# Seven block products in the first MLP, and its modulation sums moved from VectorE to ScalarE and GpSimd

## The chip, the cores and the metric

The kernel runs on one core of a Trainium2 chip. The metric is the device time of one execution in microseconds (us). The core's engines are called here by the profile's names: PE is TensorE (matmuls; PEld its weight loads), DVE is VectorE, ACT is ScalarE, POOL is GpSimd, and SP is SyncE, which here only issues DMA transfers. Each engine works through its own instructions in a fixed order and waits on semaphores for the others.

## What is computed

Two transformer blocks run one after the other on x (512 tokens, 1024 wide, float32). In outline:

```python
# first block
x = x + attention_one(rmsnorm(x, attn_norm_g)) @ w_out
hid = square(relu(rmsnorm(x, mlp_norm_g) @ w_up))      # 512 x 4096
x = x + hid @ w_down                                   # the product that is changed
# second block: six modulation rows of x's condition c, and two of the context's
mod_x = silu(c) @ w_mod + b_mod                        # 1024 x 6144
mod_c = silu(c_ctx) @ w_mod + b_mod
x = x + gt1 * rmsnorm(mix(modulate(x), modulate(ctx)) @ w_out_2)
x = x + gt2 * rmsnorm(square(relu(modulate(x) @ w_mlp_in)) @ w_mlp_out)
```

All matmuls are float32 to almost full precision: each operand is split in a high and a low part, and three matmuls (high by high, high by low, low by high) add up in PSUM.

## The kernel before

**Order.** The phases follow each other: `attention_one`, `dense_one` (the output projection, the first block's MLP, and beside it the modulation rows and the context's keys and values), `attention_two`, `dense_two` (the second projection and MLP). A scheduler lays the instructions of each engine in a fixed order, ahead of the run, by a model of their durations; work of a later part that is ready may stand before work of an earlier one. Nothing is reordered on the chip. SP issues nearly all loads, in one queue; POOL issues the small transfers and the spills.

**Splits.** `split` (L147, L148) copies a tile on ACT to its high part and subtracts on DVE to get the low part. Weights come 512 KB at a time in one of two raw buffers, and their two parts go into rings of five tiles, `wh` and `wl` (`weights`, `fetch` L169, `parts`). `mm3` (L152 to L154) issues the three matmuls. For the first four up tiles of an MLP, POOL does the low part (`WPJ`).

**First block's MLP (`mlp`).** The 4096 hidden columns are 32 tiles of 128, in four groups of eight. `up(j)` makes one tile: 24 matmuls of 512 columns (the first five in two halves of 256), ReLU on ACT (L843), the square on DVE (L844), and a split. After eight of them a down phase multiplies the group by its rows of `w_down`: four token tiles by two halves of the output, 192 matmuls. `evac2` (L975, DVE) adds each result, times the square of the norm's factor, to x, which stays in SBUF (`xa`).

**Modulation (`mods`).** A generator that `extra` advances two steps after each up tile and each eviction. A step loads 128 rows by 1024 columns of `w_mod` (L893) into one of two buffers and adds them, scaled by silu(c), to an accumulator on DVE (L896 the first, L898 the others); for the first two of six column blocks there is a second accumulator for the context. A finished accumulator is split, summed over partitions by matmuls with ones (L910, L911), gets its bias (L912) and gain (L916) on DVE, and goes to DRAM through POOL's queue (L906, L915, L918).

**Second block's MLP (`mlp_seven`).** For three of its four groups the down product is done in seven block products (Strassen's scheme in Winograd's form): hidden tiles and tokens form a 2 x 2 block matrix, rows of `w_mlp_out` and output halves another. DVE makes four sums of hidden blocks per pair of tiles (L1301 to L1304) and the splits are longer; POOL makes the differences of weight blocks (L1365, `less`), eight of 128 x 1024 in a group; seven products of 24 matmuls each go to PSUM pairs and from there to sums Y (L1355 on ACT in the first group, L1357 on DVE after that). At the end `join` (L1389, POOL) makes the four output blocks of the sums. The last group is plain.

## Time and profile before

| | |
|---|---|
| median of 3 runs | 1255.91 us (1252.36 to 1256.43) |
| the profiled execution's own time | 1260.07 us |
| its span in the trace | 1258.3 us, 16992 instructions |
| HBM | 143.24 MB read, 6.36 MB written, 119 GB/s over the span |
| first block's MLP in the trace | 277 to 661 us |
| second block's MLP in the trace | 903 to 1254 us |

Times in the trace count from the start of the span. A line number such as L148 is a line of the kernel; a helper that many parts call, as `split`, has one line for all, and there the tile's name tells the parts apart (m1u is the first MLP's up weight, m1d its down weight, m1hid its hidden tile, m2 the second's; the ending h or l is the high or low part). Matmuls overlap in PE's pipeline, so the length of one is more than the distance to the next. The chain of work that ended last is a PE chain through the second MLP.

### The profile page before, as it was taken

How to read it: one execution, taken by the hardware profiler on the slowest of the kernel's cores; microseconds unless marked ns; L12 is line 12 of the kernel's file. 1: busy time of each engine (PE TensorE's matmuls, PEld its weight loads, DVE VectorE, ACT ScalarE, POOL GpSimd, SP SyncE). 2: the span in 40 equal slices, each digit the busy share in tenths (PEclk: the TensorE clock that was granted, in tenths of full speed). 3: DMA queues.
4: the chain of work that ended last, by engine and by line, in shares of the span. 5: the costliest groups of instructions: out<-in, count | busy, mean ns of one | idle time of the engine just before them, and what ended most of it. 6: DMA issues, size and time to landing. Idle time of an engine off the chain costs nothing. (4 is left out here: it accounts for less than half of the span.)

```text
span 1258.3 us, 16992 instructions
## 1 busy us (share of the span) xinstructions
PE 1213.5 (96%) x6316; PEld 1017.5 (81%) x6316; DVE 844.6 (67%) x1410; ACT 567.3 (45%) x1068; POOL 355.1 (28%) x370
## 2 busy tenths in 40 slices
PE   7899999999999999999999999999899999999997
PEld 6898888779888878888889878777798888888885
DVE  3799766597898854346355557574868678777744
ACT  5576656434223313225254546463546454343431
POOL 2787552252010000000014124030642504205502
PEclk9899999999999999999999999999999999999999
DMA  6222222365678734134145311215443643524421
GB/s 165 64 60 53 57 63 68 101 183 154 197 220 258 240 119 138 67 101 135 67 151 157 84 53 52 85 38 201 124 162 102 185 123 117 147 81 134 150 68 67
DMA packets 151707, 150.71 MB, mean 120 GB/s; under 512 B 14345, under 2 KB 115480, under 8 KB 151624
## 3 DMA queue, kind: packets, MB, share of 16 engines
q1 hardware_dynamic: 147224, 139.41, 36.4%
q0 software_dynamic: 4400, 10.22, 2.6%
q8 instruction: 49, 0.80, 0.3%
q14 instruction: 34, 0.28, 0.1%
HBM read 143.24 MB, written 6.36 MB: 119 GB/s over the span
## 5 line engine op out<-in xcount | busy, mean ns | idle before, releaser
L1365 POOL TENSOR_TENSOR m2d<-m2d,m2d 128x1024 f32<-128x1024 f32 x24 | 71.2, 2981 | 162.2 <-DVE m2w220l L148 51.5
L898 DVE SCALAR_TENSOR_TENSOR macc<-mod,silu_c,macc 128x1024 f32<-128x1024 f32 x56 | 76.1, 1369 | 15.5 <-DMA mod<-in_w_mod_dram 15.2
L975 DVE SCALAR_TENSOR_TENSOR xa<-m1d,r,xa 128x512 f32<-128x512 f32 x32 | 23.8, 746 | 37.5 <-PE m1d L154 37.5
L918 POOL DMA_DIRECT2D modrows<-mrow x8 | 3.9, 492 | 146.4 <-DVE mrow L916 91.9
L147 ACT ACTIVATE m2hid<-m2sq 128x512 fp32r<-128x512 f32 (+1 forms) x32 | 17.6, 551 | 49.1 <-DVE m2sq L1328 49.1
L147 ACT ACTIVATE m1hid<-m1sq 128x512 fp32r<-128x512 f32 x32 | 20.0, 630 | 38.3 <-DVE m1sq L844 38.3
L148 DVE TENSOR_TENSOR npl<-t,nph 128x512 fp32r<-128x512 f32 x32 | 21.7, 682 | 16.4 <-ACT nph L147 16.3
L194 POOL TENSOR_SCALAR p<-p,d 128x512 f32<-128x512 f32 x8 | 14.0, 1752 | 57.1 <-DVE d L1116 27.3
L148 DVE TENSOR_TENSOR m2hid<-m2sq,m2hid 128x512 fp32r<-128x512 f32 (+1 forms) x32 | 24.3, 760 | 6.0 <-ACT m2hid L147 5.8
L181 POOL TENSOR_SCALAR w<-w,g_attn 128x384 f32<-128x384 f32 x20 | 25.8, 1297 | 9.1 <-DMA w<-in_w_in_dram 6.7
L148 DVE TENSOR_TENSOR m1hid<-m1sq,m1hid 128x512 fp32r<-128x512 f32 x32 | 22.0, 687 | 9.1 <-ACT m1hid L147 9.1
L683 DVE TENSOR_REDUCE mb<-sb 128x1 f32<-128x128 f32 (+3 forms) x32 | 15.6, 487 | 16.5 <-PE sb L680 16.4
L1115 ACT ACTIVATE p<-s,m 128x512 f32<-128x512 f32 x32 | 22.0, 688 | 5.8 <-DVE m L1113 5.8
L1069 POOL TENSOR_TENSOR tb<-G,nam 128x256 f32<-128x256 f32 x24 | 17.8, 774 | 22.1 <-DVE m L1109 12.5
L685 ACT ACTIVATE pb<-sb,mb 128x128 f32<-128x128 f32 (+3 forms) x32 | 16.8, 525 | 16.0 <-DVE mb L683 15.7
L843 ACT ACTIVATE m1re<-m1up 128x512 f32<-128x512 f32 x32 | 18.6, 583 | 10.1 <-PE m1up L154 9.8
L204 POOL TENSOR_SCALAR nc_0ss<-nc_0ss 128x1 f32<-128x1 f32 x1 | 0.2, 187 | 80.5 <-ACT nc_0x L256 80.5
L152 PE MATMUL pj<-w_0h,xnT 128*128 128x384 f32 (+1 forms) x48 | 18.0, 376 | 4.9 <-ACT pjs L407 3.9
L147 ACT ACTIVATE nph<-t 128x512 fp32r<-128x512 f32 x32 | 19.0, 595 | 7.5 <-PE t L1126 7.2
L981 POOL DMA_DIRECT2D xspill<-xa x4 | 2.6, 655 | 70.0 <-DVE xa L975 69.9
L844 DVE SCALAR_TENSOR_TENSOR m1sq<-m1up,m1re 128x512 f32<-128x512 f32 x32 | 21.8, 683 | 0.1
L1328 DVE SCALAR_TENSOR_TENSOR m2sq<-m2up,m2sq 128x512 f32<-128x512 f32 x32 | 21.9, 684 | 0.0
(2017 smaller groups left out, 4679.7 us busy)
## 6 DMA issues: line engine op xcount, KB each, us to landing
mod<-in_w_mod_dram SPq DMA_DIRECT2D x48, 512.0 KB, 4.6
m2d<-in_w_mlp_out_dram SPq DMA_DIRECT2D x44, 512.0 KB, 3.7
m1u<-in_w_up_dram SPq DMA_DIRECT2D x32, 512.0 KB, 4.3
m1d<-in_w_down_dram SPq DMA_DIRECT2D x32, 512.0 KB, 3.6
m2u<-in_w_mlp_in_dram SPq DMA_DIRECT2D x32, 512.0 KB, 4.1
w<-in_w_in_dram SPq DMA_DIRECT2D x16, 512.0 KB, 4.2
w<-in_w_in_dram SPq DMA_DIRECT2D x48, 128.0 KB, 2.6
o1w<-in_w_out_dram SPq DMA_DIRECT2D x8, 512.0 KB, 3.8
```

The lines of the kernel that those rows point to most:

```text
L147: self.nc.scalar.activation(out=hi, in_=src, func=AF.Copy)
L148: (eng or self.nc.vector).tensor_tensor(out=lo, in0=src, in1=hi.bitcast(F32), op=ALU.subtract)
L152: mm(out=out, lhsT=lh, rhs=rh, start=start, stop=False)
L181: eng.tensor_scalar(out=rv[:, i], in0=rv[:, i], scalar1=g, scalar2=None, op0=ALU.mult)
L843: ac(out=r, in_=acc, func=AF.Relu)
L844: nc.vector.scalar_tensor_tensor(out=s, in0=acc, scalar=0.0, in1=r, op0=ALU.max, op1=ALU.mult)
L898: nc.vector.scalar_tensor_tensor(out=accs[s], in0=rw, scalar=sc[:, s, k:k + 1], in1=accs[s], op0=ALU.mult, op1=ALU.add)
L975: nc.vector.scalar_tensor_tensor(out=x[t][:, cols], in0=acc, scalar=r2[:, t:t + 1], in1=x[t][:, cols], op0=ALU.mult, op1=ALU.add)
L1069: nc.gpsimd.tensor_tensor(out=tb[:, h, y], in0=G[:, h, ::-1, o:o + 32][:, :, ::-1], in1=nam[:, y, :].unsqueeze(1).to_broadcast([P, 8, 32]) ...
L1115: ac(out=pr, in_=s, func=AF.Exp, bias=m[:, 2:3], accum_out=den[:, 0:1])
L1328: nc.vector.scalar_tensor_tensor(out=s, in0=acc, scalar=0.0, in1=s, op0=ALU.max, op1=ALU.mult)
L1365: pt(out=o, in0=x, in1=z, op=ALU.subtract)
```

## The change

The first block's MLP now goes through `mlp_seven` too, which both blocks share in a new form; the old `mlp` goes away. With that:

- Three of the first block's four groups use seven products; the last group is plain. The evictions of a group go to sums Y in SBUF instead of x; product 1 is added to two sums, and `joined` needs ten additions on POOL instead of fourteen. The operand sums are made in place.
- To make room, x is written to DRAM after the output projection and comes back (four loads of 512 KB) during the last group, where DVE adds the sums to it.
- The modulation works in twelve column blocks of 512 instead of six of 1024, with four buffers. ACT scales each loaded tile and POOL adds it to the accumulator. `extra` advances the generator three steps, after each up tile and each product's eviction.
- During the first MLP the products have PSUM banks 0 to 3, transposes and modulation bank 4, and the up tiles 5 to 7.
- In the first MLP the weight blocks have five buffers (`RB_1`), in the second six (`RB_2`, as before).

Parts that are written but not used by this kernel (`last_seven`) are left out here.

```diff
@@ constants
+MRAW = 4
+RB_2 = 6
+RB_1 = 5
+MSTEPS = 3
@@ mods
+        def raw(name):
+            return ep.tile([P, 512], F32, tag="mraw", name=name, bufs=MRAW)
...
-        for cb in range(6):
+        for blk in range(12):
+            cb, hf = blk // 2, blk % 2
...
-                rw = ep.tile([P, D], F32, tag="mraw", name=f"mod{cb}{k}", bufs=2)
-                nc.sync.dma_start(out=rw, in_=a["w_mod_2"][0, k * P:(k + 1) * P, cb * D:(cb + 1) * D])
+                rw = raw(f"mod{blk}{k}")
+                nc.sync.dma_start(out=rw, in_=a["w_mod_2"][0, k * P:(k + 1) * P, wcols])
                 for s in range(len(accs)):
+                    gain = sc[:, s, k:k + 1]
                     if k == 0:
-                        nc.vector.tensor_scalar(out=accs[s], in0=rw, scalar1=sc[:, s, k:k + 1], scalar2=None, op0=ALU.mult)
-                    else:
-                        nc.vector.scalar_tensor_tensor(out=accs[s], in0=rw, scalar=sc[:, s, k:k + 1], in1=accs[s],
-                                                       op0=ALU.mult, op1=ALU.add)
+                        ac(out=accs[s], in_=rw, func=AF.Copy, scale=gain)
+                        continue
+                    term = raw(f"term{blk}{k}") if s + 1 < len(accs) else rw
+                    ac(out=term, in_=rw, func=AF.Copy, scale=gain)
+                    nc.gpsimd.tensor_tensor(out=accs[s], in0=accs[s], in1=term, op=ALU.add)
                 yield
...
@@ dense_one, evac1
+                    nc.gpsimd.dma_start(out=self.xspill[t * P:(t + 1) * P, :], in_=x[t])
...
+        self.banks(a=(0, 1, 2, 3), t=(4,), s=(5, 6, 7))
...
+    def mlp_one(self, hT, g, r2):
...
+        def extra():
+            for _ in range(MSTEPS):
+                next(gen, None)
+        last_ups, last_plain, _ = self.mlp_seven(hT, a["w_up"], a["w_down"], hidx, Y, RB_1, extra, "m1")
+        for _ in gen:
+            pass
...
+            if j == NJ - 4:
+
+                for t in range(NT):
+                    x[t] = xtile(f"xa2{t}")
+                    nc.sync.dma_start(out=x[t], in_=self.xspill[t * P:(t + 1) * P, :])
+                    for half in range(2):
+                        cols = slice(half * 512, half * 512 + 512)
+                        nc.vector.scalar_tensor_tensor(out=x[t][:, cols], in0=Y[((2, 3), (4, 5))[t // 2][half]][t % 2],
+                                                       scalar=r2[:, t:t + 1], in1=x[t][:, cols], op0=ALU.mult, op1=ALU.add)
...
@@ mlp_seven
+            self.split(hi[:, 1:3].rearrange("p o t -> p (o t)"), lo[:, 1:3].rearrange("p o t -> p (o t)"), s)
+            a11, a21, a12, a22 = st[:, 0, 0:256], st[:, 0, 256:512], st[:, 1, 0:256], st[:, 1, 256:512]
+            tt(out=a22, in0=a21, in1=a22, op=ALU.add)
+            tt(out=a21, in0=a11, in1=a21, op=ALU.subtract)
+            tt(out=a11, in0=a22, in1=a11, op=ALU.subtract)
+            tt(out=a12, in0=a12, in1=a11, op=ALU.subtract)
+            self.split(hi[:, 3:7], lo[:, 3:7], st.rearrange("p f (x t) -> p (f x) t", x=2))
...
+        def down(g):
+            def into(*ns):
+                def evac(tau, acc):
+                    for n, first in ns:
+                        if g == 0 and first:
+                            ac(out=Y[n][tau], in_=acc, func=AF.Copy)
+                        else:
+                            tt(out=Y[n][tau], in0=acc, in1=Y[n][tau], op=ALU.add)
+                    extra()
+                return evac
+            b11 = blocks(g, 0, 0)
+            times(g, 1, 0, b11, into((6, True), (2, True)))
+            t1 = blocks(g, 0, 1)
+            less(t1, t1, b11)
+            times(g, 5, S1, t1, into((5, True)))
+            t2 = blocks(g, 1, 1)
+            less(t2, t2, t1)
+            times(g, 6, S2, t2, into((6, False)))
+            b21 = blocks(g, 1, 0)
+            times(g, 2, A12, b21, into((2, False)))
+            less(b21, t2, b21)
+            times(g, 4, A22, b21, into((4, True)))
+            b22 = blocks(g, 1, 1)
+            times(g, 3, S4, b22, into((3, True)))
+            b12 = blocks(g, 0, 1)
+            less(b22, b22, b12)
+            times(g, 7, S3, b22, into((7, True)))
...
+        for g in range(NG - 1):
+            for j in range(g * G, (g + 1) * G):
+                if j == NSP:
+                    self.rings["s"] = s_banks
+                up(j, True)
+                extra()
+            down(g)
```

## Rows read from the trace of the kernel before

**Rows 1.** The page's first part: busy time, share of the span, instructions.
```profile
PE 1213.5 (96%) x6316; PEld 1017.5 (81%) x6316; DVE 844.6 (67%) x1410; ACT 567.3 (45%) x1068; POOL 355.1 (28%) x370
```
**Rows 2.** Stretches: length, busy by engine (instructions), granted clock, DMA share, GB/s.
```profile
253.00:298.00 45.00, 41.85 (x246) 37.00 (x245) 37.92 (x37) 15.59 (x22) 26.03 (x20) 0.96 0.61 181
277.00:332.00 55.00, 51.85 (x342) 47.83 (x341) 48.39 (x52) 21.63 (x31) 18.20 (x17) 0.97 0.57 170
332.00:431.00 99.00, 99.00 (x426) 79.89 (x425) 81.86 (x88) 31.74 (x39) 8.21 (x14) 1.00 0.73 229
431.00:476.00 45.00, 43.19 (x179) 34.39 (x178) 29.37 (x31) 10.11 (x11) 1.94 (x4) 0.96 0.50 154
1039.00:1078.00 39.00, 39.00 (x170) 31.79 (x169) 36.34 (x30) 14.30 (x16) 22.30 (x8) 1.00 0.39 123
```
**Rows 3.** Timeline of ACT: ReLU evictions (start, length, engine, line, operation, tiles).
```profile
514.95 0.58 ACT L843 ACTIVATE m1re<-m1up 128x512 f32<-128x512 f32 x1
520.53 0.58 ACT L843 ACTIVATE m1re<-m1up 128x512 f32<-128x512 f32 x1
...
611.77 0.58 ACT L843 ACTIVATE m1re<-m1up 128x512 f32<-128x512 f32 x1
...
1122.63 0.58 ACT L1327 ACTIVATE m2sq<-m2up 128x512 f32<-128x512 f32 x1
...
1206.17 0.58 ACT L1327 ACTIVATE m2sq<-m2up 128x512 f32<-128x512 f32 x1
```
**Rows 4.** Timeline around TensorE's two waits (in brackets: idle before, what ended it).
```profile
278.33 5.69 DVE L898 SCALAR_TENSOR_TENSOR macc<-mod,silu_c,macc 128x1024 f32<-128x1024 f32 x2
...
279.60 3.34 POOL L148 TENSOR_TENSOR m1u2l<-m1u,m1u2h 128x1024 fp32r<-128x1024 f32 x1
...
284.77 0.63 PE L216 MATMUL n_2t<-ident,xg 128*128 128x128 f32 x4 [3.15 <-DVE xg L940]
...
444.42 0.50 PE L152 MATMUL m1d<-m1d100h,m1hid 128*128 128x512 f32 x1 [1.81 <-DVE xa L975]
```
**Rows 5.** Tiles macc and mrow: count, shortest/median/longest in ns, first and last start.
```profile
L898 DVE SCALAR_TENSOR_TENSOR macc<-mod,silu_c,macc x56: 1261/1278/3386, 257.4 to 448.4; 128x1024 f32<-128x1024 f32 x56
...
L906 POOL DMA_DIRECT2D mrow<-in_b_mod_dram x8: 484/490/609, 290.0 to 438.5; - x8
```
**Rows 6.** Prices: POOL's sum and difference, ACT's copy, DVE's operand sum.
```profile
L940 POOL TENSOR_TENSOR xg<-xa,g_mlp x4: 1263/1280/2277, 241.7 to 260.9; 128x512 f32<-128x512 f32 x4
...
L1365 POOL TENSOR_TENSOR m2d<-m2d,m2d x24: 2394/3261/3447, 927.4 to 1147.7; 128x1024 f32<-128x1024 f32 x24
...
L147 ACT ACTIVATE m1hid<-m1sq 128x512 fp32r<-128x512 f32 x32 | 20.0, 630 | 38.3 <-DVE m1sq L844 38.3
...
1041.02 0.42 DVE L1301 TENSOR_TENSOR g_post<-m2sq 128x256 f32<-128x256 f32 x1
```
**Rows 7.** Timeline of DVE and POOL in a down phase of the second block.
```profile
1063.53 3.04 DVE L148 TENSOR_TENSOR m2w170l<-m2d,m2w170h 128x1024 fp32r<-128x1024 f32 x1
...
1065.65 3.19 POOL L1365 TENSOR_TENSOR m2d<-m2d,m2d 128x1024 f32<-128x1024 f32 x1 [0.16 <-POOL m2d L1365]
...
1066.49 0.68 DVE L1357 TENSOR_TENSOR y<-m2p,y 128x512 f32<-128x512 f32 x1
1067.09 2.83 DVE L148 TENSOR_TENSOR m2w171l<-m2d,m2w171h 128x1024 fp32r<-128x1024 f32 x1
...
1069.35 9.52 POOL L1365 TENSOR_TENSOR m2d<-m2d,m2d 128x1024 f32<-128x1024 f32 x3 [0.52 <-DMA m2d<-in_w_mlp_out_dram]
```
**Rows 8.** Timeline: a weight split, and first uses of split weights on TensorE.
```profile
498.34 1.23 DVE L148 TENSOR_TENSOR m1d200l<-m1d,m1d200h 128x1024 fp32r<-128x1024 f32 x1 [2.30 <-ACT m1d200h L147]
...
519.60 0.40 PE L152 MATMUL m1d<-m1d200h,m1hid 128*128 128x512 f32 x1
...
1074.09 0.40 PE L152 MATMUL m2p<-m2w171h,m2hid 128*128 128x512 f32 x1
```
**Rows 9.** DMA issues: a load of 256 KB, median us to landing.
```profile
w<-in_w_in_dram SPq DMA_DIRECT2D x6, 256.0 KB, 3.9
```

More of the change, by code (lines that the diff above doesn't have):

```diff
@@ L900, in mods @@
                 yield
             for (s, gname, dst) in todo[cb]:
-                ah = self.part("wh", f"mh{cb}{s}")
-                al = self.part("wl", f"ml{cb}{s}")
-                self.split(ah, al, accs[s])
-                row = ep.tile([P, D], F32, tag="xr", name=f"mrow{cb}{s}", bufs=2)[0:1, :]
-                nc.gpsimd.dma_start(out=row, in_=a["b_mod_2"][:, cb * D:(cb + 1) * D])
-                for hf in range(2):
-                    pt = self.ps("t", f"mp{cb}{s}{hf}")
-                    cols = slice(hf * 512, hf * 512 + 512)
-                    nc.tensor.matmul(out=pt, lhsT=ones, rhs=ah[:, cols], start=True, stop=False)
-                    nc.tensor.matmul(out=pt, lhsT=ones, rhs=al[:, cols], start=False, stop=True)
-                    nc.vector.tensor_tensor(out=row[:, cols], in0=pt[0:1, :], in1=row[:, cols], op=ALU.add)
+                hl = self.part("wh", f"mh{blk}{s}")
@@ new lines, in mods @@
+                self.split(hl[:, 0:512], hl[:, 512:1024], accs[s])
+                row = raw(f"mrow{blk}{s}")[0:1, :]
+                nc.gpsimd.dma_start(out=row, in_=a["b_mod_2"][:, wcols])
+                pt = self.ps("t", f"mp{blk}{s}")
+                nc.tensor.matmul(out=pt, lhsT=ones, rhs=hl[:, 0:512], start=True, stop=False)
+                nc.tensor.matmul(out=pt, lhsT=ones, rhs=hl[:, 512:1024], start=False, stop=True)
+                nc.vector.tensor_tensor(out=row, in0=pt[0:1, :], in1=row, op=ALU.add)
@@ L924, in dense_one @@
     def dense_one(self):
[L925 to L929 removed]
+        tc, nc, a = self.tc, self.nc, self.a
         g = self.gp.tile([P, 2, D], F32, tag="g", name="g_mlp")
@@ L976, in evac2 @@
                                            op0=ALU.mult, op1=ALU.add)
-            if grp == NJ // 8 - 1 and half == 1:
+            if half == 1:
                 if t == 0:
@@ L1230, in squares @@
+    def squares(self, src, ss, second, name, tag="sqr"):
         nc = self.nc
         j = self.ep.tile([P, 512], F32, tag=tag, name=name, bufs=2)
-        nc.scalar.activation(out=j, in_=src, func=AF.Square, accum_out=ss[:, half:half + 1])
-        if half == 0:
+        nc.scalar.activation(out=j, in_=src, func=AF.Square, accum_out=ss[:, second:second + 1])
+        if not second:
             nc.gpsimd.tensor_scalar(out=ss[:, 0:1], in0=ss[:, 0:1], scalar1=1.0 / D, scalar2=EPS, op0=ALU.mult, op1=ALU.add)
@@ new lines, in dense_two @@
+            hidx = self.ep.tile([P, 7168], F32R, tag="hidx", name="m2hidx", bufs=1)
+            more = self.ep.tile([P, D], F32, tag="more", name="m2more", bufs=1)
+            Y = {n: [b[:, h * 512:h * 512 + 512] for h in range(2)]
+                 for n, b in ((2, y[0]), (3, y[1]), (4, y[2]), (5, y[3]), (6, more), (7, gg[:, 0, :]))}
+            self.row(gg[:, 1, :], 5)
+            last_ups, last_plain, last_seven = self.mlp_seven(hT, a["w_mlp_in_2"][0], a["w_mlp_out_2"][0], hidx, Y, RB_2, lambda: None, "m2")
@@ new lines, in dense_two, with fetch_x, done @@
+            x = {}
+            ss2 = [self.small("ss", f"ss2{t}") for t in range(NT)]
+            def fetch_x(ts):
+                for t in ts:
+                    x[t] = self.ep.tile([P, D], F32, tag="rb", name=f"xc{t}", bufs=RB_2)
+                    nc.sync.dma_start(out=x[t], in_=self.xspill2[t * P:(t + 1) * P, :])
+            def done(t, half, first, z):
+                r = self.squares(z, ss2[t], 0 if first else 1, f"sk{half}{t}", "sqr")
+                nc.vector.tensor_tensor(out=z, in0=z, in1=gg[:, 1, half * 512:half * 512 + 512], op=ALU.mult)
+                if not first:
+                    for _, c in self.post(x[t], [Y[((2, 3), (4, 5))[t // 2][i]][t % 2] for i in range(2)], r):
+                        nc.sync.dma_start(out=self.out[0, t * P:(t + 1) * P, c], in_=x[t][:, c])
@@ L1426, with evac @@
+            last_ups(False, lambda j: None)
+            fetch_x(range(NT))
+            def evac(half, t, acc):
+                z = Y[((2, 3), (4, 5))[t // 2][half]][t % 2]
+                nc.vector.tensor_tensor(out=z, in0=acc, in1=z, op=ALU.add)
+                done(t, half, half == 0, z)
+            last_plain(evac)
 _INS = ['x', 'attn_norm_g', 'w_in', 'b_forget', 'q_norm_a', 'k_norm_a', 'sink_logits', 'q_norm_b', 'k_norm_b', 'w_out',
```

400 lines of the change are left out of this document (182 added, 218 removed).

## The prediction

> **What bounds the kernel now.** I read the page first: TensorE is busy 96% of the span, VectorE (DVE) 67%, GpSimd (POOL) 28% [rows 1]. Shares over the span hide the stages, so I then cut the first block's MLP into stretches [rows 2]. From 332 to 431 TensorE is busy all 99 us, DVE 81.9 and POOL 8.2 of them. TensorE's matmuls set the time there, DVE is close behind, and POOL has room.
>
> TensorE's pace comes from the ReLU evictions: two neighbouring up tiles are 5.58 us apart [rows 3], and one has 24 matmuls of 512 columns, so a matmul costs 0.2325 us. From the last ReLU of one group of eight tiles to that of the next, the plain first block takes 91.24 us and the second block, with seven products, 83.54 us [rows 3].
>
> TensorE waits twice in the stretch: 3.15 us for DVE's xg and 1.81 us for DVE's eviction [rows 4]. The first shows a trap. DVE took 5.69 us for two modulation steps of 1.28 us (the median, [rows 5]) because POOL's split of m1u2, 3.34 us, ran beside them; xg stood behind them, and TensorE behind xg. The order on each engine is fixed ahead, so a collision that it does not foresee becomes a wait of this kind. The stretches around the two waits have a mean granted clock of 0.97 over 55 us and 0.96 over 45 us [rows 2], between the levels of 1.2 and 2.4 GHz, where 332 to 431 has 1.00: that is 1.65 and 1.8 us more. Together: 3.15 + 1.81 + 3.45 = 8.4 us.
>
> **The change, part by part.**
>
> *TensorE.* In three of four groups seven products of 24 matmuls replace 192: 3 x 24 x 0.2325 = 16.7 us less. The periods differ by 7.7 us a group instead of 5.58, but the plain one also holds context and modulation work and clock loss, so I keep the count.
>
> *DVE.* Removed: 64 modulation terms of at most 1.28 us [rows 5], 82 us. Added in three groups: for each of 12 pairs of tiles four operand sums of 0.42 and a split of 1.23, with 0.42 + 0.68 where 2 x 0.68 was, 2.7 us; six more weight splits of 1.23 a group; 18 more evictions and sums with x of 0.68 net (42 for 24) [rows 6 to 8]: 32 + 22 + 12 = 66 us. DVE's own work falls by only some 16 us. But the steps that held xg go, and I count the 8.4 us as gained; if other work delays the same places it is 0.
>
> *ACT.* 128 terms at 0.63 us [rows 6] are 81 us, with splits and copies of the products some 120 us. ACT was busy 31.7 + 10.1 of 144 us [rows 2]. I take 0; a term that waits for its load holds the weight splits behind it in ACT's queue, which is counted below.
>
> *POOL.* 112 sums of 1.26 us [rows 6] are 141 us, 24 differences of 2.39 us [rows 6] are 57 us, and 42 instead of 21 small transfers of 0.49 us [rows 5]; x is written out once more, four more issues.
>
> *POOL beside DVE* decides. In the second block's products the two take turns [rows 7]: DVE's split ends at 1066.57, POOL's difference, begun at 1065.65, ends 2.27 us after that, and DVE's next split ends 1.08 us after POOL. Evictions from PSUM keep 0.68 us beside POOL. So a POOL sum and a DVE instruction with two SBUF inputs exclude each other. Three turns took 9.52 us, 3.17 each, a little less than 2.27 + 1.08; scaled to that the exclusive parts are 2.15 us for a difference, 1.08 for a sum of 512, and 1.02, 0.51 and 0.26 us for DVE's 1024, 512 and 256 columns.
> - An up phase needs 8 x 1.02 + 4 x (0.26 + 0.51 + 4 x 0.26 + 1.02) = 19.5 us, a down phase 14 x 1.02 + 8 x 2.15 = 31.5 us.
> - Sums in a phase: a step with two accumulators holds two of the four buffers through a load (3.9 us, [rows 9]), 1.26 us of ACT and 2.52 of POOL, so four sums come per 7.7 us: 17 in what is left of the first up phase after 298 (33 us), 23 in the second. In a down phase POOL has 39 - 8 x 2.39 = 19.9 us, 16 sums. Before 298 it has 45 - 26.0 us [rows 2], 15 sums. The last 25 fall in the third up phase.
> - Demand against TensorE's time: first up 15.4 + 18.4 in 33; each down 31.5 + 17.3 in 39; second up 19.5 + 24.8 + 4 (accumulator splits) in 47; third up 19.5 + 27 + 4 in 44.7. Excess: 0.8 + 9.8 + 1.3 + 9.8 + 5.8 = 27.5 us.
> - What the queues carry: a weight split was done 20.0 us before its use in the plain block (499.57 to 519.60), 4.2 us in the second block's down phase (1069.92 to 1074.09) [rows 7, 8]. Both kinds of phase occur, so I take the middle, 12.1 us.
>
> That leaves 27.5 - 12.1 = 15.4 us of TensorE idle and, in the two down phases at least, clock losses of 1.73 us each: 18.9 us. Bounds: 0 where all is carried, 31 us where nothing is.
>
> The Trainium skill has this as a rule (SBUF — State Buffer, "Who interferes with whom"): the port pair that both share is an exclusive lock, and a DVE instruction with two SBUF inputs contends for it with a GpSimd one that reads SBUF. It speaks against the change, and the turns of [rows 7] agree with it.
>
> *Transfers.* 96 loads of half the size for 48, 12 more blocks of w_down and four reloads of x: 64 more issues on SP's queue. The stretch 332 to 431 had the DMA engines 0.73 busy [rows 2] with no wait of TensorE; I take 0. A load that waits for a buffer that a POOL sum frees holds the weight loads behind it: the same excess, not a second one.
>
> *Edits at nothing.* The second block's two more evictions a group, 1.36 us, fit in DVE's 36.3 of 39 us [rows 2]; without that cover up to 2.7 us. Its joins fall from 14 to 10 on POOL, a gain that I don't count. Four PSUM banks for five leave an eviction of 0.68 us one product, 5.58 us; it is late only where DVE is, which is the excess again. x comes back while three up tiles are still to run.
>
> **Sum:** -16.7 - 8.4 + 18.9 = -6.2 us. Against the profiled execution's own 1260.07 us this is 1253.9; the median of the runs is 1255.91, 4.2 us lower, so 1249.7, given as 1250 us.
>
> **Rivals.**
> - *The sums hide*: 0 for the exclusion, -25.1, 1231 us; with the old waits left, 1239. For: 81.9 of 99 us on DVE did not stop TensorE [rows 2]. Against: POOL has some 220 us to do in the stretch, and more in its turns.
> - *The gain is eaten*: the queues carry only the 4.2 us of a down phase: -25.1 + 27.5 - 4.2 + 3.5 = +1.7, 1257.6 us.
> - *Slower: the same exclusion with the sums early.* Each call hands out three steps, 113 steps in 1.7 groups. If the queues keep that pace, 97 sums (104.8 us) and 91.7 us of other demand stand in 140.5 us of TensorE from 298 to the middle of the second down phase: 56 over, 12.1 carried, 3.5 of clock: -25.1 + 47.4 = +22.3, 1278 us. It turns the sign where the excess passes 25.1 + 12.1 - 3.5 = 33.7 us. For: the old terms ran at that pace, 257.4 to 448.4 [rows 5]. Against: four buffers and POOL's own 1.26 us spread the sums.
> - *The products save less than counted* needs dearer matmuls; the 83.54 us period of the same products [rows 3] speaks against it.
>
> **How the numbers follow.** A measurement of this kernel can tell about 0.3%, 3.8 us, from no change. Chances: the forecast's zone (1241 to 1252) 0.34, hidden (below 1241) 0.14, eaten (1252 to 1260) 0.18, slower 0.34 (0.20 up to 1275, 0.14 beyond). So faster 0.48, same 0.18, slower 0.34. The range 1234 to 1280 leaves out some 0.06 below and 0.12 above; the likeliest case's own range is 1234 to 1252.
>
> **What would show it.** Right: a period near 84 us between last ReLUs of the first block once the sums are done; POOL over 0.7 busy to about 500, its sums stretched from 1.26 towards 2 us; DVE's splits of 1.23 us at 2 to 3 us; TensorE idle in the first two down phases, released by DVE's splits, and a granted clock below 1.00 there. Wrong: TensorE without idle from 298 to 545 (hidden), over 34 us of idle there (slower), or idle that transfers or ACT end while POOL is free.

## The result and the profile after

The changed kernel takes 1421.53 us (median of 6 runs, 1419.86 to 1425.09), the kernel before 1256.57 beside it: 1.132 times as long, 95% interval 1.1295 to 1.1344. The forecast was 1250 us, with 1280 as the end of its range. The measured time is 171.5 us above the forecast.

The page of the changed kernel, to be read beside [rows 1]: busy times, three of its lines of slices, and the two groups that matter most.

```profile
PE 1232.1 (87%) x6244; PEld 1017.2 (72%) x6244; DVE 887.7 (63%) x1465; ACT 685.4 (48%) x1244; POOL 582.4 (41%) x537
...
PE   7889999945446497499999998999999999999996
...
POOL 3877521567668755740430123232054230502401
PEclk9999999977667798799999999999999999999998
...
L860 POOL TENSOR_TENSOR macc<-macc,mod 128x512 f32<-128x512 f32 x84 | 114.9, 1368 | 40.3 <-ACT mod L859 25.4
L868 PE MATMUL mp<-mh,ones 128*128 128x512 f32 x16 | 11.3, 707 | 129.9 <-ACT mh L151 129.9
```

A slice is 35 us. From the ninth slice to the seventeenth, where POOL makes the modulation sums, TensorE is at 0.4 to 0.6 with two slices excepted, and its clock is down as well. Later it is at 0.9 again. The last row has the place: TensorE sat idle 129.9 us before the `mp` matmuls, which add a finished accumulator over the partitions, and what ended the idle time was ACT's split of that accumulator, `mh`.

Four stretches of the same kernel, columns as in [rows 2]:

```profile
298.00:332.00 34.00, 8.03 (x38) 6.41 (x37) 13.94 (x14) 16.64 (x24) 27.57 (x23) 0.60 0.23 69
332.00:431.00 99.00, 52.53 (x200) 39.96 (x200) 46.20 (x46) 52.99 (x77) 66.58 (x60) 0.74 0.33 99
431.00:476.00 45.00, 20.46 (x66) 14.24 (x65) 13.97 (x12) 20.35 (x29) 35.28 (x27) 0.71 0.53 170
...
545.00:612.00 67.00, 40.12 (x138) 29.34 (x137) 36.47 (x39) 29.03 (x38) 46.00 (x33) 0.77 0.44 137
```

Where the kernel before had TensorE busy 99 of 99 us [rows 2], it is now busy 52.5. But look at the others: DVE 46, ACT 53, POOL 67, DMA 0.33. No engine is full; POOL comes nearest, 35.3 of 45 us in the next stretch. A stretch with no full engine is not explained by one engine's amount of work; the reading taken here is a chain in which the engines wait for one another by turns. From 298 to 612 TensorE's busy times add up to 179.9 of 314 us, so it idled 134 us.

One turn of that chain, from the timelines of POOL, DVE, ACT and TensorE in turn (in brackets: idle before, and what ended it):

```profile
373.80 1.27 POOL L860 TENSOR_TENSOR macc<-macc,term 128x512 f32<-128x512 f32 x1
375.03 1.27 POOL L860 TENSOR_TENSOR macc<-macc,mod 128x512 f32<-128x512 f32 x1
376.25 1.25 POOL L860 TENSOR_TENSOR macc<-macc,term 128x512 f32<-128x512 f32 x1
377.48 1.25 POOL L860 TENSOR_TENSOR macc<-macc,mod 128x512 f32<-128x512 f32 x1
382.96 1.62 POOL L860 TENSOR_TENSOR macc<-macc,term 128x512 f32<-128x512 f32 x1 [4.24 <-ACT term L859]
...
373.80 5.48 DVE L152 TENSOR_TENSOR m1hidx<-m1sq,m1hidx 128x512 fp32r<-128x512 f32 x1 [2.43 <-ACT m1hidx L151]
380.69 0.43 DVE L1264 TENSOR_TENSOR m1sq<-m1sq 128x256 f32<-128x256 f32 x1
...
381.15 1.06 ACT L151 ACTIVATE m1hidx<-m1sq 128x1024 fp32r<-128x1024 f32 x1 [4.10 <-DVE m1sq L1264]
388.31 0.72 ACT L859 ACTIVATE mod<-mod,silu_c 128x512 f32<-128x512 f32 x1
390.02 0.63 ACT L151 ACTIVATE mh<-macc 128x512 fp32r<-128x512 f32 x1 [0.99 <-POOL macc L860]
...
390.70 0.80 PE L868 MATMUL mp<-mh,ones 128*128 128x512 f32 x1 [16.57 <-ACT mh L151]
```

POOL runs four sums back to back. DVE's split of 512 columns, 0.68 us when left alone, begins with the first and ends 0.55 us after the last: it is held for 5.48 us. DVE's operand sums come after it, so ACT waits 4.10 us to split them. The next terms stand behind that split in ACT's queue, so POOL, which has nothing left to add, waits 4.24 us for a term. Then come the remaining terms and sums of the block (one term after 2.61 us of waiting for its load, at 387.55), ACT's `mh`, and only then TensorE, after 16.57 us of idle. Such waits are 12 in this profile, the longest 25.4 us.

The loads are a link of the chain too. Over the whole kernel ACT's terms waited 81 us for them, as the page has it:

```profile
L859 ACT ACTIVATE mod<-mod,silu_c 128x512 f32<-128x512 f32 x84 | 59.6, 720 | 53.2 <-DMA mod<-in_w_mod_dram 49.6
...
L859 ACT ACTIVATE term<-mod,silu_c 128x512 f32<-128x512 f32 x28 | 20.1, 718 | 31.6 <-DMA mod<-in_w_mod_dram 31.5
```

Two more lines, the sums (tile `macc`) and the matmul after the wait (tile `mp`):

```profile
L860 POOL TENSOR_TENSOR macc<-macc,mod x84: 1249/1284/2863, 300.2 to 597.6; 128x512 f32<-128x512 f32 x84
...
L868 PE MATMUL mp<-mh,ones x16: 398/793/796, 324.9 to 599.6; 128*128 128x512 f32 x16
```

A sum takes 1.28 us in the median: its price was right. The matmul after a wait takes 793 ns where 398 is the shortest: after the idle time it runs at the lower of the clock's two levels, 1.2 in place of 2.4 GHz.

### The profile page after: what moved, and what is told of

Read it like the earlier page. It is cut to its first block, busy times and chain, and to the rows that moved or that the text cites. A ratio compares the mean times of both kernels' runs of the same rounds, so it can differ in the third digit from the quotient of the medians.

```text
span 1418.4 us, 17524 instructions
## 1 busy us (share of the span) xinstructions
PE 1232.1 (87%) x6244; PEld 1017.2 (72%) x6244; DVE 887.7 (63%) x1465; ACT 685.4 (48%) x1244; POOL 582.4 (41%) x537
## 5 line engine op out<-in xcount | busy, mean ns | idle before, releaser
L860 POOL TENSOR_TENSOR macc<-macc,mod 128x512 f32<-128x512 f32 x84 | 114.9, 1368 | 40.3 <-ACT mod L859 25.4
L868 PE MATMUL mp<-mh,ones 128*128 128x512 f32 x16 | 11.3, 707 | 129.9 <-ACT mh L151 129.9
L1280 POOL TENSOR_TENSOR m1d<-m1d,m1d 128x1024 f32<-128x1024 f32 x24 | 66.6, 2782 | 88.9 <-DMA m1d<-in_w_down_dram 42.9
L859 ACT ACTIVATE mod<-mod,silu_c 128x512 f32<-128x512 f32 x84 | 59.6, 720 | 53.2 <-DMA mod<-in_w_mod_dram 49.6
L860 POOL TENSOR_TENSOR macc<-macc,term 128x512 f32<-128x512 f32 x28 | 36.9, 1319 | 24.0 <-ACT term L859 23.7
L1251 DVE SCALAR_TENSOR_TENSOR m1sq<-m1up,m1sq 128x512 f32<-128x512 f32 x32 | 21.9, 685 | 38.6 <-ACT m1sq L1250 38.6
L859 ACT ACTIVATE term<-mod,silu_c 128x512 f32<-128x512 f32 x28 | 20.1, 718 | 31.6 <-DMA mod<-in_w_mod_dram 31.5
L151 ACT ACTIVATE m2hid<-m2sq 128x512 fp32r<-128x512 f32 (+2 forms) x26 | 17.7, 681 | 33.0 <-DVE m2sq L1251 28.5
L152 DVE TENSOR_TENSOR npl<-t,nph 128x512 fp32r<-128x512 f32 x32 | 21.7, 681 | 16.4 <-ACT nph L151 16.3
L152 DVE TENSOR_TENSOR m1hid<-m1sq,m1hid 128x512 fp32r<-128x512 f32 (+2 forms) x26 | 22.6, 873 | 13.5 <-ACT m1hid L151 13.5
L152 DVE TENSOR_TENSOR m2hid<-m2sq,m2hid 128x512 fp32r<-128x512 f32 (+2 forms) x26 | 24.6, 958 | 9.3 <-ACT m2hid L151 9.3
L152 DVE TENSOR_TENSOR m1hidx<-m1sq,m1hidx 128x256 fp32r<-128x256 f32 (+2 forms) x18 | 24.0, 1339 | 9.8 <-ACT m1hidx L151 9.8
L684 DVE TENSOR_REDUCE mb<-sb 128x1 f32<-128x128 f32 (+3 forms) x32 | 15.5, 486 | 16.7 <-PE sb L681 16.6
```

The costliest lines, as they stand in the source:

```text
L151: self.nc.scalar.activation(out=hi, in_=src, func=AF.Copy)
L152: (eng or self.nc.vector).tensor_tensor(out=lo, in0=src, in1=hi.bitcast(F32), op=ALU.subtract)
L859: ac(out=term, in_=rw, func=AF.Copy, scale=gain)
L860: nc.gpsimd.tensor_tensor(out=accs[s], in0=accs[s], in1=term, op=ALU.add)
L1251: nc.vector.scalar_tensor_tensor(out=s, in0=acc, scalar=0.0, in1=s, op0=ALU.max, op1=ALU.mult)
L1280: pt(out=o, in0=x, in1=z, op=ALU.subtract)
```

## The experiments

Eighteen kernels, each timed against the kernel before on the same chip (medians 1254.5 to 1257.2 us there). Where the text gives no other base, a variant is one edit of the changed kernel. The scheduler lays out each variant anew, so a difference between two holds their orders too. Lines of `...` mark what an edit shown here leaves out.

### The first theory: TensorE's own order at mp

The profile suggests that TensorE, whose order is fixed, is held by the `mp` matmuls. The rivals were the exclusion of POOL and DVE (B), and SP's queue with the ring of four load buffers (C).

Modulation on DVE, in halves of 512 (the first term of a block too):
```
...
-  ac(out=term, in_=rw, func=AF.Copy, scale=gain)
-  nc.gpsimd.tensor_tensor(out=accs[s], in0=accs[s], in1=term, op=ALU.add)
+  nc.vector.scalar_tensor_tensor(out=accs[s], in0=rw, scalar=gain, in1=accs[s], op0=ALU.mult, op1=ALU.add)
```


> The changed kernel with the modulation terms and sums as one instruction each on DVE again (halves of 512, same loads, same rings, same pace of three steps a call, same seven products). Theory A (the modulation chain of load, ACT term, POOL sum, ACT and DVE split is too long for its place, and TensorE's own order holds it at the mp matmuls): the chain is shorter by two engines, TensorE's idle before mp falls from 130 us to under 30, time 1240 to 1275 us. Rival B (POOL sums and DVE exclude each other): no sums are left, time 1231 to 1250 us. Rival C (the four load buffers and SP's queue: modulation loads hold the weight loads): loads and buffers are as in the changed kernel, time over 1340 us.

Measured 1358.01 us, ratio 1.0811 (1.0763 to 1.0858): A and B missed, C's range holds it. That DVE was simply full in this form (a row below) is another reading.

The kernel before with `mods()` of the changed kernel, and at both places in its `extra`:
```
-            next(gen, None)
+            for _ in range(2):
+                next(gen, None)
...
```


> The kernel before with nothing but its modulation as in the changed kernel (halves of 512, ACT terms, POOL sums, four buffers, rows through the same buffers), four half steps a call in place of two whole ones; no seven products, x stays in SBUF. Theory A: the loss belongs to the modulation alone, TensorE waits 90 to 150 us for mh at the mp matmuls, time 1360 to 1430 us. Rival B (exclusion): DVE has no block differences beside it here, time 1265 to 1300 us. Rival D (the loss needs the seven products, whose block differences stand on POOL between the sums): 1256 to 1275 us.

Measured 1327.41 us, 1.0553 (1.0520 to 1.0586). Blocks of 512 with terms on ACT and sums on POOL cost the plain kernel 70 us, so a good part of the loss needs no seven products. The time lies below A's range and above those of B and D.

Three empty steps before `mh`:
```
+            for _ in range(3):
+                yield
             for (s, gname, dst) in todo[cb]:
                 hl = self.part("wh", f"mh{blk}{s}")
```


> The changed kernel with three empty steps (one call, so one up tile or one product's half more of TensorE work) between a block's last sum and its split and mp matmuls. Nothing else changes, the number of sums, loads and matmuls is the same. Theory A: TensorE's idle before mp falls from 130 us to 30 to 80, and the clock rises, time 1290 to 1360 us. Rival B: the same sums beside the same DVE work, time over 1400 us. Rival C: the buffers are held as long or longer, time over 1400 us.

Measured 1391.78 us, 1.1074 (1.1035 to 1.1113): 30 us returned, outside every range.

Without the `mp` matmuls:
```
-  nc.tensor.matmul(out=pt, lhsT=ones, rhs=hl[:, 0:512], start=True, stop=False)
-  nc.tensor.matmul(out=pt, lhsT=ones, rhs=hl[:, 512:1024], start=False, stop=True)
-  nc.vector.tensor_tensor(out=row, in0=pt[0:1, :], in1=row, op=ALU.add)
+  nc.vector.tensor_tensor(out=row, in0=hl[0:1, 512:1024].bitcast(F32), in1=row, op=ALU.add)
```


> The changed kernel without its 32 mp matmuls (the sum over the partitions is left out, the bias is added to the low part of the split instead); terms, sums, splits, rings, loads and rows stay. Theory A (TensorE's own order holds it): 1240 to 1275 us. Rival B: over 1400 us, since the sums are all there. Rival C (weight slots taken by mh, loads behind modulation loads): the idle goes to the up tiles and products, time over 1340 us.

Measured 1417.78 us, 1.1268 (1.1232 to 1.1305). Theory A falls: the matmuls that showed the wait are gone, and the time stays, as B and C have it. Its waits of TensorE (total, count, longest):

```profile
PE m1up L156 <- ACT m1u4h L151: 27.2, 1, 27.2
PE m1p L156 <- ACT m1w050h L151: 17.4, 1, 17.4
PE m1p L156 <- ACT m1w020h L151: 16.2, 1, 16.2
PE m1p L156 <- ACT m1w070h L151: 14.4, 1, 14.4
```

The idle has moved to the weights whose splits stand behind `mh` in ACT's queue. The row that named `mp` named the first instruction that came late, not the reason.

### How fast the steps are handed out

Theory E: 113 steps are asked for in 38 calls, some 140 us of TensorE's work, and POOL can't supply them so fast. Spread over the 66 calls of the three groups, `steps` 2.4 after an up tile and 1.3 after a half product:
```
-            for _ in range(MSTEPS):
+            owed[0] += steps
+            while owed[0] >= 1:
+                owed[0] -= 1
                 next(gen, None)
...
```


> The changed kernel with its 113 modulation steps spread over all 66 calls of the three groups (2.4 steps on average after an up tile, 1.3 after a half product) in place of three steps in each of the first 38 calls. Nothing is added or left out. Theory E (demand: the steps are asked for in some 140 us of TensorE's work, while POOL alone has 112 sums of 1.3 us and 16 differences of 2.8 us there, 190 us; every queue is in order, so what POOL is late by reaches the weight splits): TensorE's idle falls from 130 us to under 40, time 1240 to 1290 us. Rival C (latency: a block's chain takes 20 to 30 us with four buffers whatever the pace, 12 blocks take some 270 us, more than the 252 us of the three groups): time 1310 to 1400 us. Rival B (POOL and DVE exclude each other): the same sums beside the same work, over 1380 us.

Measured 1391.71 us, 1.1072 (1.1032 to 1.1111). E falls. C's range holds it, and so does B's (over 1380 us): the two are not told apart. The trace has the clearest row on the exclusion (POOL, then DVE, then TensorE):

```profile
379.31 2.42 POOL L1285 TENSOR_TENSOR m1d<-m1d,m1d 128x1024 f32<-128x1024 f32 x1
381.67 1.31 POOL L861 TENSOR_TENSOR macc<-macc,term 128x512 f32<-128x512 f32 x1
...
385.42 1.26 POOL L861 TENSOR_TENSOR macc<-macc,mod 128x512 f32<-128x512 f32 x1
...
379.25 8.52 DVE L153 TENSOR_TENSOR m1w040l<-m1d,m1w040h 128x1024 fp32r<-128x1024 f32 x1 [0.22 <-ACT m1w040h L152]
...
387.82 0.50 PE L158 MATMUL m1p<-m1w040l,m1hid 128*128 128x512 f32 x1 [2.55 <-DVE m1w040l L153]
```

A weight split of 1.23 us lasts 8.52 us, through a difference and four sums, and TensorE waits for it.

The same pace with the DVE form of the first experiment:
```
+                    nc.vector.scalar_tensor_tensor(out=accs[s], in0=rw, scalar=gain, in1=accs[s], op0=ALU.mult, op1=ALU.add)
...
+            owed[0] += steps
...
```

> As the run before with the modulation terms on DVE (one instruction for term and sum), same pace of 2.4 and 1.3. Theory E: DVE's demand (47 of 50 us busy where TensorE idled in the DVE form at three steps a call) is spread as well, time 1235 to 1265 us. Rival C: the loads and buffers are the same, over 1300 us. Rival B: no sums on POOL, 1231 to 1250 us. If it is over 1290 us, DVE itself has too much to do in the three groups, whatever the pace.

Measured 1316.73 us, 1.0476 (1.0437 to 1.0514). The number fits C and the last sentence of the expectation, that DVE itself has too much to do. For the latter speaks the DVE form at three steps, where DVE, the third busy time of the row, had 47.6 of 50 us:

```profile
300.00:350.00 50.00, 33.92 (x148) 26.20 (x147) 47.60 (x67) 16.25 (x22) 11.66 (x11) 0.83 0.44 136
```

Slower still, into the last group, in `hook` and after the last up tiles:
```
-UP_STEPS = 2.4
-DOWN_STEPS = 1.3
+UP_STEPS = 2.0
+DOWN_STEPS = 1.1
...
         def hook(j):
+            extra()
...
```

> The changed kernel with 2.0 steps an up tile and 1.1 a half product, going on through the eight up tiles of the last group, what is left then drained. Theory E: as slow as POOL can follow, 1240 to 1280 us, no more than the run with 2.4 and 1.3. Rival C: over 1300 us. A third outcome, a lump of idle where the rest is drained ahead of the context products, would show as one wait of 10 to 30 us.

Measured 1362.96 us, 1.0841 (1.0809 to 1.0874): 59 us returned, the best of the forms with ACT and POOL, but far from E's 1280 and in C's range.

The eight blocks whose rows are first read in the second block moved to the last, plain group, the other four spread over the three groups, with empty steps before `mh`; in `hook` and `evac2`:
```
...
+            extra(LATE_STEPS, 999)
...
```


> The changed kernel with the same ACT terms and POOL sums handed out later: the four blocks with two accumulators (the rows that the first block itself needs) over the 66 calls of the three groups, 1 step an up tile and 0.7 a half product, three empty steps before each mh; the other eight blocks, whose rows are first read in the second block, in the last, plain group at 5.5 steps a call. Theory E (supply against demand in the seven-product groups: POOL 56 sums and 24 differences in 252 us, 0.55 busy): 1240 to 1275 us, idle in the three groups under 15 us. Rival L or S at whatever pace: over 1300 us. A lump may appear in the last group, where 5.5 steps of one accumulator ask POOL for 5.6 us in 5.6 us.

And with DVE's share in it:
```
+                    if blk >= 4 or s == 0:
+                        nc.vector.scalar_tensor_tensor(out=accs[s], in0=rw, scalar=gain, in1=accs[s], op0=ALU.mult, op1=ALU.add)
+                        continue
...
```


> As the run before with the work shared by engine: in the first four blocks the first accumulator on DVE (one instruction of 0.95 us a term), the second by ACT and POOL; the eight late blocks on DVE. Theory E: DVE has 0.7 of its time taken without modulation and 28 terms more in 252 us, POOL 28 sums, 1235 to 1255 us, below the kernel before. Rival: DVE's and POOL's mutual exclusion makes even these late, 1270 us or more.

Measured 1406.58 us, 1.1198 (1.1154 to 1.1243), and 1381.47 us, 1.0982 (1.0937 to 1.1027). E fails in both, about half by a new lump: in the first TensorE idles 44 us from 300 to 600 and 53 us from 600 to 750. Of that run:

```profile
550.00:600.00 50.00, 40.35 (x164) 31.84 (x164) 39.08 (x40) 17.26 (x22) 27.98 (x21) 0.91 0.33 110
600.00:650.00 50.00, 22.80 (x77) 17.19 (x78) 19.60 (x30) 22.34 (x37) 23.44 (x23) 0.64 0.44 132
```

From 300 to 600 TensorE now has 256 of 300 us, where I expected under 15 us of idle; in the last group, at 5.5 steps a call, it loses more than half of a stretch, and again no engine is full. Later is no better if the steps still come in a crowd.

### Which part of the modulation

The sums left out:
```
-  nc.gpsimd.tensor_tensor(out=accs[s], in0=accs[s], in1=term, op=ALU.add)
```


> The changed kernel at its own pace of three steps a call without the 112 sums on POOL (the accumulators keep the first term only, so seven eighths of the modulation product are left out); loads, ACT terms, splits, mp matmuls, rows and buffers stay. Theory E: POOL has 45 us left in place of 190, TensorE's idle falls from 130 us to under 30, time 1235 to 1270 us. Rival C (loads, buffers, ACT's queue): still over 1320 us. Rival B: 1231 to 1250 us.

Measured 1324.87 us, 1.0541 (1.0505 to 1.0577): 97 us less. It is the largest part found, yet E and B missed and C's 1320 holds: something else is left.

The whole modulation product left out, a floor:
```
-  nc.sync.dma_start(out=rw, in_=a["w_mod_2"][0, k * P:(k + 1) * P, wcols])
...
-  ac(out=term, in_=rw, func=AF.Copy, scale=gain)
-  nc.gpsimd.tensor_tensor(out=accs[s], in0=accs[s], in1=term, op=ALU.add)
...
-  self.split(hl[:, 0:512], hl[:, 512:1024], accs[s])
...
-  nc.tensor.matmul(out=pt, lhsT=ones, rhs=hl[:, 0:512], start=True, stop=False)
-  nc.tensor.matmul(out=pt, lhsT=ones, rhs=hl[:, 512:1024], start=False, stop=True)
-  nc.vector.tensor_tensor(out=row, in0=pt[0:1, :], in1=row, op=ALU.add)
```


> The changed kernel without the modulation product: its 96 loads, terms, sums, splits and mp matmuls are left out, the rows are written from the bias alone. It gives the floor for the seven products with x through DRAM. If the terms of the forecast for TensorE are right (16.7 us fewer matmuls, 8.4 us of old waits and clock gone): 1225 to 1240 us, with no wait over 5 us from 298 to 545. If the products themselves bring waits or save less: over 1248 us.

Measured 1254.77 us, 0.9988 (0.9971 to 1.0006). A surprise, taken up below: even with no modulation at all the changed kernel only equals the kernel before with all of it.

The loads left out:
```
-  nc.sync.dma_start(out=rw, in_=a["w_mod_2"][0, k * P:(k + 1) * P, wcols])
+  rw = hT[k // 4][:, k % 4, 0, :].bitcast(F32)
...
```


> The changed kernel at its own pace without the 96 modulation loads: ACT's terms read a part of the normed activations that lies in SBUF, every term takes a buffer of the ring of four (so the numbers are not the modulation's); sums, splits, mp matmuls, rows stay. Theory L (the loads: SP's queue, the ring and their latency): SP's queue is free, time under 1300 us. Theory S (POOL's sums are the slow step, and the run without them has shown 97 us): 1340 to 1400 us, TensorE idle and released by ACT's mh as before.

Measured 1398.3 us, 1.1131 (1.1098 to 1.1163): theory S's range. Loads and sums both left out:
```
...
+  rw = hT[k // 4][:, k % 4, 0, :].bitcast(F32)
...
-  nc.gpsimd.tensor_tensor(out=accs[s], in0=accs[s], in1=term, op=ALU.add)
```

> The changed kernel at three steps a call without the 96 modulation loads and without the 112 POOL sums (ACT's terms read the normed activations, the accumulators keep the first term); terms, splits, mp matmuls and rows stay. Theory F (two limits of one in-order chain, the ring of loads on SP and the sums on POOL, each enough by itself): 1255 to 1285 us, close to the floor of 1255. Rival G (the ACT terms, the mh splits in the weights' ring and the rows cost by themselves): 1300 us or more.

Measured 1284.97 us, 1.0223 (1.0191 to 1.0254), the upper end of F. So, from the floor: 1254.8; with terms, splits, `mp` and rows 1285.0 (+30); with the loads 1324.9 (+40); with the sums 1421.5 (+97). Sums before loads, the sums are 113 and the loads 23. The loads cost less where the sums are slow already: that fits two links of one chain. The first 30 us have a likely cause in a stretch of the kernel with both left out, where ACT is the fourth busy time of the row:

```profile
332.00:431.00 99.00, 89.80 (x367) 68.62 (x366) 75.01 (x84) 90.66 (x142) 40.38 (x41) 0.98 0.37 107
```

ACT is busy 90.7 of 99 us. At three steps a call the terms, beside what ACT had to do before, nearly fill it.

How much of the sums' 97 us is POOL holding DVE? The pages give a bound. DVE runs 1465 instructions with the sums and without them, and is busy 887.7 and 871.4 us: held for 16.3 us more in all. The sums themselves take 151.8 us where 112 at the shortest, 1.25 us, are 140: 12 us more. Together these holds are 28 us. In a fixed order a hold delays the end by no more than itself; a new order and a lower clock can add to that. The reading that fits is that the larger part of the 97 us is the sums' own time as a link between terms and splits. It is argued from these totals.

The loads issued by POOL, in place of SP:
```
-  nc.sync.dma_start(out=rw, in_=a["w_mod_2"][0, k * P:(k + 1) * P, wcols])
+  nc.gpsimd.dma_start(out=rw, in_=a["w_mod_2"][0, k * P:(k + 1) * P, wcols])
```


> The changed kernel with the 96 modulation loads issued by POOL in place of SP; nothing left out, same ring, same pace. Theory H (SP's order: waiting modulation loads hold the weight loads behind them): the weight loads go ahead, 1340 to 1390 us although POOL has 96 issues of 0.5 to 1 us more. Rival S (POOL's sums are the slow step and SP's order only follows): POOL has more to do, 1425 to 1500 us.

Measured 1452.73 us, 1.155 (1.1508 to 1.1593). H falls, S holds: taking the loads out of SP's order frees nothing on balance. But they now stand behind POOL's sums, so a smaller gain from SP's order could hide in this; the loads left out altogether returned 23 us. TensorE's largest wait grew by 27 us:

```profile
PE mp L868 <- ACT mh L151: 156.8, 12, 29.1
```

POOL's block differences moved to DVE, sums left on POOL:
```
-  pt(out=o, in0=x, in1=z, op=ALU.subtract)
+  (tt if name == "m1" else pt)(out=o, in0=x, in1=z, op=ALU.subtract)
```


> The changed kernel at three steps a call with the first block's 24 differences on DVE, sums still on POOL, nothing left out. If POOL's total time holds it (190 us of work asked for in 140 us): 1360 to 1390 us. If each DVE instruction that falls into a run of sums waits for its end: the differences on DVE are held too, 1410 to 1440 us.

Measured 1406.51 us, 1.1215 (1.1178 to 1.1253): 15 us less, where POOL was relieved of 66.6 us (24 of 2.78 us) over the three groups. The value lies between the two ranges: POOL's amount of work is not the limit by itself, and the differences on DVE do not lose either.

### Why the seven products save nothing

The floor kernel without POOL's block differences:
```
+            if name == "m1":
+                return
```


> The floor kernel (no modulation product) without the 24 differences of weight blocks on POOL in the first block, so that its products multiply the plain blocks. If DVE's splits, 14 of which take 2.4 to 3.4 us beside the differences, are what makes TensorE wait 10 us at the first products and lowers its clock: 1238 to 1248 us. If not: 1252 to 1257 us.

Measured 1233.96 us, 0.9809 (0.9776 to 0.9843): 20.8 us less, more than expected. In the floor kernel, TensorE's waits, one of them, then ACT, DVE and POOL around it:

```profile
PE m1p L156 <- ACT m1hidx L151: 9.6, 3, 3.5
...
429.64 0.80 PE L156 MATMUL m1p<-m1w151h,m1hidx 128*128 128x512 f32 x1 [3.48 <-ACT m1hidx L151]
...
428.53 1.06 ACT L151 ACTIVATE m1hidx<-m1sq 128x1024 fp32r<-128x1024 f32 x1 [6.81 <-DVE m1sq L1247]
...
421.79 3.42 DVE L152 TENSOR_TENSOR m1w121l<-m1d,m1w121h 128x1024 fp32r<-128x1024 f32 x1
...
425.58 2.46 DVE L1246 TENSOR_TENSOR m1sq<-m1sq 128x256 f32<-128x256 f32 x1
...
421.66 2.46 POOL L1263 TENSOR_TENSOR m1d<-m1d,m1d 128x1024 f32<-128x1024 f32 x1 [20.43 <-DVE m1w120l L152]
425.34 2.42 POOL L1263 TENSOR_TENSOR m1d<-m1d,m1d 128x1024 f32<-128x1024 f32 x1 [1.21 <-issue]
```

A split of 1.23 us takes 3.42 and an operand sum of 0.42 takes 2.46, each beside a difference of POOL, where a group's products wait for their operand sums. ACT waits 6.81 us for the last of these sums, and TensorE 3.48 us for ACT. Without the differences the 9.6 us of waits are gone and the granted clock is 1.00 from 298 to 545, where the floor kernel has 0.97.

The differences on DVE, still without modulation:
```
-  pt(out=o, in0=x, in1=z, op=ALU.subtract)
+  (tt if name == "m1" else pt)(out=o, in0=x, in1=z, op=ALU.subtract)
```


> The floor kernel (no modulation product) with the first block's 24 differences of weight blocks on DVE in place of POOL. Theory B (exclusion: DVE's splits are held through a whole run of POOL's instructions): DVE's splits go back to 1.25 us, the 30 us of differences fit, 1234 to 1244 us. Rival V (DVE has no room, 0.8 busy already): 1250 us or more.

And the kernel before without its modulation product:
```
-  nc.sync.dma_start(out=rw, in_=a["w_mod_2"][0, k * P:(k + 1) * P, cb * D:(cb + 1) * D])
...
-  nc.vector.scalar_tensor_tensor(out=accs[s], in0=rw, scalar=sc[:, s, k:k + 1], in1=accs[s],
...
-  self.split(ah, al, accs[s])
...
-  nc.tensor.matmul(out=pt, lhsT=ones, rhs=ah[:, cols], start=True, stop=False)
...
```

> The kernel before without its modulation product (48 loads, terms, sums, splits, mp matmuls left out, rows from the bias alone): the floor to compare the floor of the seven products with. If modulation was hidden in the kernel before but for its 32 matmuls (7.4 us) and the old waits (8.4 us): 1238 to 1250 us, and the seven products then save nothing or lose. If the seven products save 10 us or more by themselves: 1262 us or more, which would need modulation to have cost less than nothing, or 1254 to 1257 us if it was hidden altogether.

Measured 1244.54 us, 0.9926 (0.9900 to 0.9952), and 1240.76 us, 0.9868 (0.9834 to 0.9902): the first half a us above B's range and short of V's, the second in the range of "hidden but for its 32 matmuls and the old waits". With the differences on DVE two of the three waits for `m1hidx` stay, 3.2 us each: the differences and a weight split now stand between DVE's operand sums. So 10.6 of the 20.8 us that the differences cost stay (by medians) when they no longer hold DVE from POOL, and that half is not the exclusion. One stretch of the plain floor and the same of the seven-product one, DVE the third busy time, POOL the fifth:

```profile
332.00:431.00 99.00, 99.00 (x428) 80.17 (x427) 38.22 (x43) 26.95 (x33) 0.00 (x0) 1.00 0.28 85
```
```profile
332.00:431.00 99.00, 95.29 (x403) 76.21 (x402) 78.28 (x84) 45.48 (x60) 39.77 (x32) 0.98 0.40 118
```

So without modulation on either side the seven products are 14 us slower than the plain ones as the change has them, 4 us slower with the differences on DVE (7 us by the two ratios to the kernel before), and 7 us faster only if the differences cost nothing. That the plain kernel hid its modulation well fits DVE's room: it had 61 of 99 us free there; beside the seven products it has 21.

| kernel | us | over its floor |
|---|---|---|
| plain, no modulation | 1240.8 | |
| plain, modulation on DVE (before) | 1256.6 | 15.8 |
| plain, on ACT and POOL, blocks of 512 | 1327.4 | 86.6 |
| seven products, no modulation | 1254.8 | |
| seven products, on DVE, three steps / spread | 1358.0 / 1316.7 | 103 / 62 |
| seven products, on ACT and POOL (changed) / slowest pace | 1421.5 / 1363.0 | 167 / 108 |

No version that computes everything beat the kernel before. Since the seven-product floor with all its operands lies at 1244.5 at best, there was at most 12 us to win with products of this form, and only with the modulation out of this stage.

## Why the prediction was wrong

**The sign and the size.** The forecast was -6.2 us; it was +165. The rival that ended on the other side ("the same exclusion with the sums early", 1278 us) had the right sign and place: the steps come at three a call, and the sums fall into the first two groups. Its size was wrong by 143 us, for the reason that comes next.

**The step that failed** is "POOL beside DVE", where it adds exclusive times against TensorE's time, 27.5 us of excess, and lets "what the queues carry", 12.1 us, take a part off. It came to 15.4 us of TensorE idle; the measured idle is 134. That is a sum of work, and it is right only while each engine runs ahead of the next and fills the gaps. From 332 to 431 POOL was busy 0.67 and no engine was full; TensorE's waits for `mh`, 129.9 us, are nearly all of the idle. Nor was POOL's work the limit: 66.6 us less of it returned 15 us. The reading that fits: a block's last terms, sums, split and `mp` follow one or two calls of TensorE's work, every link stands in its queue behind something that waits for TensorE, and so the queues carry almost nothing. It is argued from the queues' order; what runs show of it is that empty steps and a slower pace, with the same work, gave 30 to 59 us back. The bound of 31 us "where nothing is" carried still came from work, and so was no bound.

**ACT at 0.** The forecast took nothing for ACT's terms and counted a held split "below". A term took 0.72 us (388.31 above) where 0.63 was counted. Where loads and sums are out of the way ACT is busy 90.7 of 99 us, and terms, splits, `mp` and rows are 30 us by themselves.

**Transfers: "the same excess, not a second one".** The loads are 23 us on top of the sums and 40 us without them. That they share a chain was right; that they add nothing was not.

**The clock.** Two losses of 1.73 us were counted. The granted clock was 0.60, 0.74, 0.71 and 0.77 in the four stretches above. Against the floor's span (1253.5) the changed kernel's is 164.9 us longer: by the two pages TensorE is idle 128.9 us more (186.3 against 57.4) and busy 36.0 us more (1232.1 against 1196.1). Of the 36.0 up to 22.6 are the lengths of the `mp` matmuls, which the floor kernel leaves out; the rest fits matmuls at the lower level.

**TensorE, -16.7.** The count is right, the cover is not. From the last ReLU of the first group to that of the second, the plain kernel without modulation takes 89.4 us (412.48 to 501.86) and the seven products without differences 84.0 (410.50 to 494.51): 5.4 us a group, the forecast's 5.58. With the differences on POOL it is 90.0 us (413.02 to 503.05). The 83.54 us of [rows 3], which I set against that rival, was read from a group of the second block; why the same differences cost less there was not tried.

**-8.4 for the old waits.** This fits: the waits of [rows 4] are gone, and the plain kernel without modulation is 15.8 us faster, as much as the 8.4 and 32 matmuls of 0.2325 us (7.4) add up to. In the changed kernel it can't be seen beside the new waits.

**DVE's own work.** I had 66 us added. Over the whole kernel DVE is busy 751.9 us in the plain floor and 818.4 in the seven-product one without differences: 66.5 us. With POOL's differences it is 855.1: 36.7 us more of the same instructions held by POOL. The instructions were counted well, their time beside POOL was not.

**The turns of [rows 7]** were read as POOL and DVE taking one each. The Trainium skill (SBUF — State Buffer, "Who interferes with whom") has the port pair as an exclusive lock, for which a DVE instruction with two SBUF inputs contends with a GpSimd one that reads SBUF. The rows agree: in the floor kernel the split of 3.42 us ends 1.09 us after the difference beside it. What they add is that the other need not get the next turn: the split of 8.52 us sat through five of POOL's instructions. By the totals above (28 us of holds) this is the smaller part of the sums' 97 us. Exactly how much, no run here separates: a sum on POOL that doesn't exclude DVE was not tried, nor an order laid out with the longer durations.

Of the signs named in advance, the one for "slower" came: over 34 us of idle (107 of 247 us from 298 to 545), and the clock below 1.00 with it. POOL was busy 148 of 202 us from 298 to 500, as named. The sums were not stretched towards 2 us, and what released TensorE was ACT's splits, not DVE's. The period of 84 us can't be read here, since the sums reach into the second down phase and the last group is plain.

## What to carry to other kernels

Moving work to an idle engine need not help if the work stays one link of a chain that the busy engine waits for; it adds a hand-over. Cost such a chain by its latency from the last thing it waits for to the first thing that waits for it, and compare that with the time between its places in the program; sums of busy time did not give the time here, where no engine was full. Before giving POOL anything that reads two tiles of SBUF, see how full DVE is: here differences of 67 us on POOL cost 21 and on DVE 11, and sums of 152 us on POOL cost 97, of which at most 28 us are counted above as holds. When a wait is named by an instruction, leave that instruction out and see if the time goes; here it moved to the next one and the time stayed.

## What the runs showed of the hardware

A DVE instruction with two SBUF inputs can be held through several POOL instructions in a row, 5.48 us for a split of 0.68 and 8.52 us for one of 1.23. At other places the two took turns: three operand sums of DVE, 0.42 us each alone, took 1.37 us each beside a run of sums,

```profile
308.04 1.37 DVE L1261 TENSOR_TENSOR m1sq<-m1sq 128x256 f32<-128x256 f32 x1
309.44 1.37 DVE L1262 TENSOR_TENSOR m1sq<-m1sq 128x256 f32<-128x256 f32 x1
310.85 1.37 DVE L1263 TENSOR_TENSOR m1sq<-m1sq 128x256 f32<-128x256 f32 x1
```

one for each sum of POOL (1.44 us at 309.09 and 310.50). What decides between the two was not found.
